# GpSimd scales the first head pair's softmax rows

## The chip, the core and the metric

One core of a Trainium2 chip runs one launch of the kernel. The metric is the time of the launch on the device in microseconds (us). The engines are TensorE (PE, with its weight loads as PEld), VectorE (DVE), ScalarE (ACT), GpSimd (POOL) and SyncE (SP, which here only issues DMAs).

## The reference, cut to what matters

One layer of a hybrid trunk is computed for 512 new frames of one stream and 64 next frames of a running one. Half of the heads are a state-space scan (SSD), the other half are latent attention (MLA), and a dense feed-forward network (FFN) follows. The change lies in the softmax of the attention:

```python
def block(args):
    ql, qr, qp = args
    s = (jnp.einsum('bqhl,bkl->bhqk', ql, keys_c, preferred_element_type=jnp.float32)
         + jnp.einsum('bqhr,bkr->bhqk', qr, keys_r, preferred_element_type=jnp.float32))
    mask = k_chunk[None, :] <= (qp // CHUNK)[:, None]
    s = jnp.where(mask, s * scale, -jnp.inf)
    pr = jax.nn.softmax(s, axis=-1).astype(keys_c.dtype)
    return jnp.einsum('bhqk,bkl->bqhl', pr, keys_c)
...
o = jnp.einsum('bthl,lhd->bthd', o_lat, p['w_uv']).reshape(b, T, MLA_WIDTH)
x = x + jnp.concatenate([y_ssd, o], axis=-1) @ p['w_out']
```

## The kernel before

The kernel runs through stages in one program: input projections and convolution, the SSD chunks, the attention, the output projection, the FFN and the final norm. Tokens lie on the free axis for most tensors (512 and 64, side by side), channels on the partitions.

In the attention the eight heads are worked in four pairs `p` (0 to 3). For a pair, `scores(p, i)` makes the scores of query block `i`: blocks 0 to 3 are 128 prompt queries each against `(i + 1) * 128` keys, one PSUM bank per head (`sc`, three banks in turn); block 4 (`sc_s`) is the 64 sample queries of both heads in one bank against 320 keys. `soft` then does four steps per head `j`: VectorE finds the negated row maximum from PSUM (L655), ScalarE exponentiates from PSUM into the SBUF tile `pr` and adds up the row sums (L656), VectorE takes the reciprocals of the sums of both heads in one instruction (L657), and the rows are multiplied by the reciprocal: head 0 by VectorE (L662), head 1 by ScalarE (L660). The exponential frees the PSUM bank for the next scores. `turn` then transposes `pr` on TensorE (`ptp`, L694), which needs the scaled rows of the query blocks that it covers, and `values` multiplies by V (`pv`, L719).

Around the first pair, which is the one that the diff touches, other work is interleaved: the second halves of the y norm (`nr_u`, `Ry`, L172 to L179), the gated SSD output scaled and split into `cat_y` for the output projection (L764, L143, L145), the splitting of the next pair's weights (`wl_pair`, L112) and copies of the next pair's queries (`qs`, L622). GpSimd has masked the SSD decay tiles (`cumb`, L515) before, and next issues the four DMAs that put the rotary part of pair 2's queries in place (`qs<-rrp`, L616).

The order of the work on each engine is written out: `ORDER_ATT` sets the order in which the pieces are made (S03 is block 3 of pair 0; the first pair goes S03, S01, S02, S00, S04), and `ISSUE` lists for each engine the numbers of its instructions in the order in which they are to be issued; `issue_in_order` turns that list into dependencies. The tiles of row sums and maxima (`sm`, `mx`) have four buffers, so the fifth block, S04, takes the buffer of S03, and the first block of pair 1 that of S01.

Of the kernel before, what the change touches and what calls it, by code (L numbers as in the profile page):

```python
# [14 lines left out]
ALU = mybir.AluOpType  # L15
# [39 lines left out]
def hybrid_layer_kernel(ctx: ExitStack, tc: tile.TileContext, a, o):  # L55
# [592 lines left out]
    def soft(p, i, scs, nk):  # L648
# [676 lines left out]
98-99 93-97 70-73 86-91 104-106 100-103 110 107-109 122-126 134-135 111-115 128-133 148-153 116-121 136-141 127  # L1325
142-147 154-169 174-175 170-171 270-274 176-221 172-173 222-269 275-370 373-420 371 421-468 372 469-634 637 641-644
638-640 657-660 635-636 665-726 737-758 661-664 763 645-652 759-760 727-736 764-766 653-656 767-818 859 761-762
819-826 860-864 833-840 827-832 865-870 841-852 871-874 853-856 875-880 857-858 881-887 904-912 888 892-899 889-891
900-903 925-926 913-921 927-934 922-924 935 939-940 936-938 949-957 964-966 941 945-948 967-968 958-963 969 942-944
970-975 987 976-979 1003 980-986 991-993 988 1004-1005 1015-1021 1006-1014 1022-1024 994-996 1025-1026 1029-1034  # L1330
1043-1045 997-998 989 1000-1002 999 1046-1054 990 1035-1039 1059-1061 1040-1042 1062-1064 1027-1028 1075-1077
1081-1092 1055-1057 1078-1080 1093-1096 1058 1097-1104 1121-1123 1071-1072 1124-1129 1065 1068-1070 1073 1105-1107
1066-1067 1074 1130-1156 1119-1120 1229-1240 1157 1108-1114 1158 1241-1245 1253-1262 1246-1247 1115-1118 1159-1161
1176-1177 1248-1252 1263-1264 1162-1175 1265 1180 1178 1181-1183 1179 1266-1268 1277-1279 1184-1187 1190-1195
1269-1276 1196-1204 1188-1189 1205-1223 1227-1228 1224-1226 1280-1297 1301-1303 1298-1300 1304-1321 1342-1343
1348-1355 1344-1347 1322-1341 1356-1511 1572 1512-1559 1575-1576 1560-1571 1577 1596-1598 1578 1573-1574 1593
1584-1585 1579 1581-1583 1602-1604 1623-1625 1594-1595 1614 1586 1605-1606 1590-1592 1611-1613 1632-1634 1587-1589
1608-1610 1607 1580 1599-1601 1620-1622 1641 1626-1628 1647-1649 1642-1643 1615-1616 1635-1637 1617-1619 1638-1640
1653 1656 1658-1667 1644-1646 1629-1631 1650-1652 1654-1655 1668-1669 1657 1682 1694-1705 1683-1693 1670-1681
1730-1741 1706-1729 1742-1748 1754-1755 1749-1753 1756-1767 1778-1785 1768-1777 1786-1885 1898-1905 1886-1897  # L1340
1906-2017 2030-2036 2018-2029 2037-2053 2066-2084 2054-2065 2085-2089 2102-2104 2090-2101 2105-2221 2234-2236
2240-2241 2222-2233 2237 2242-2248 2238-2239 2249-2725 2738-2740 2744 2726-2737 2741 2745-2751 2742-2743 2752-3229
3242-3244 3248 3230-3241 3245 3249-3255 3246-3247 3256-3733 3746-3748 3752 3734-3745 3749 3753-3759 3750-3751
3760-4189
# [5 lines left out]
101-102 125 120 126-127 119 131-133 155 134 129 135-136 140-142 149 104 152 128 150 153 170 143-144 138 145 147 151  # L1350
154 156 137 146 174 157 178 159 171-172 187 169 160 158 161-162 176 206 163 175 183 180 164 167 165-166 168 215 181
177 188 173 189 182 184 190 195 191 179 192-194 197 185-186 224 196 204 207-209 198-203 214 205 210 288 211 225
216-218 212 220 222 219 213 226 221 223 227-228 233 229-230 234 231-232 235-236 245 255 246 237 294 256 247 239 248
257 259 258 260 240 238 264 241 261 242 263 262 307 267 243 265 244 266 249 268 270 251 269 253 250 274 252 254
275-276 289 271 290 277-279 295 286 280 282 281 287 272 297 317 291 283 318 273 298 302 299 316 300 284-285 319 303
306 292-293 296 309 312 304 326 305 310 308 313 327 362 311 328 322 301 323 314 363 330 324 320 329 315 336 321 325
364 333 367 337 331-332 365 340 338 334-335 341 344 349 339 350 345 342 346 352 351 343 355 358 366 347 359 357 348
360 356 353 361 368 377 354 370-371 369 372 375-376 373-374 382 390 378 384 383 385-386 379 389 387 380 397 388 381
393 405 395 391 396 394 392 400 399 401 398 403 402 420 406 404 408 407 409 412 410 417 414 411 413 418 462 416 421
423 419 464 425 422 424 415 433 431 426 432 429 428 427 438 430 434 469 463 436 435 437 439 442 441 443 466 440 444  # L1360
451 465 446 467-468 452-453 445 447 455 454 448 473 475 456 477 476 474 457 472 470 478 458-459 449-450 479 460 481
480 461 471 482 491 487 483 496-497 484 488 498-499 489 500-502 485-486 503 510 490 515-518 522 492 504 519 506 520
507 521 508 532-535 539 546 493-495 536 547-549 505 511-512 509 523 537 529-530 524-525 513-514 531 538 540 528 550
541 566 526 542 527 551 543 545 552 544 567-568 553-554 569 555 574 570 556-559 561 575-576 560 565 577 562 578-581
571 582-583 572 563 590-591 584 592 585-586 564 598 573 599-600 593-594 587-588 601 589 603 602 595 604-607 596 610
597 608-609 620-623 611 627 612 624 613-614 625-626 619 634-636 628 637 617 638 618 629 616 615 630 641 639 631 640
633 632 654-656 642 657 643 662 658 644-647 649 663-664 648 653 665 650 666-669 659 670-671 660 651 678-679 672 680
673-674 652 686 661 687-688 681-682 675-676 689 677 691 690 683 692-695 684 698 685 696-697 708-711 699 715 700 712
701-702 713-714 707 722-724 716 725 705 726 706 717 704 703 718 729 727 719 728 721 720 742-744 730 745 731 750 746
732-735 737 751-752 736 741 753 738 754-757 747 758-759 748 739 766-767 760 768 761-762 740 774 749 775-776 769-770  # L1370
763-764 777 765 779 778 771 780-783 772 786 773 784-785 796-799 787 803 788 800 789-790 801-802 795 810-812 804 813
793 814 794 805 792 791 806 817 815 807 816 809 808 830-832 818 833 819 839 834 820-823 825 840-841 824 829 842 826
843-846 835 847-848 836 827 855-856 849 857 850-851 828 864 837 865-866 858 838 859 852-853 867 854 869 868 860
870-873 861 876 862 874 880 875 881-883 887 884 863 885 877 886 879 878 888-898
""",
    "ACT": """
0-5 8 6-7 10 9 13 11 14 12 15 17-18 16 21 19 24 20 23 40 22 25 45 26-27 52 28-33 49-50 56 34-35 37 36 60 51 41-43
38-39 64 44 46-48 53-54 68 55 57-58 72 59 61-62 76 63 65-67 77 69-71 73 92 74-75 94 79 88 78 81 104 82 90 84 116 86-87
103 85 83 100 98 80 97 89 99 102 101 96 91 126 105 93 111 109-110 156 115 95 107-108 113 122 114 112 142 117 163 106
118-119 136 127 137 134 128 140 135 124 121 120 139 129 138 141 130 123 143 131 125 150 146 149 132 210 133 145 148  # L1380
154 152 151 147 158-159 157 144 155 160-162 153 164-165 212 170 172 171 166 168 180 186 169 181 174 187 175 173 176
189 167 190 177 227 178 192 179 193 188 182 195 194 191 183 200 196 184-185 199 201 197 213 208 215-216 202-203 219
209 204 217 234 218 198 205-206 211 214 226 220 233 221 240 207 223 242 224 222 241 229 243-244 225 271 235 230 228
231 238 237 272 232 245 236 248 239 246 249-252 247 257 255 261 254 262 256 259 263 258 278 265 253 267 266 264
268-270 260 273-277 284 280-282 285 287 283 279 293 286 291 288 290 289 302 292 294 296 295 298 300 297 301 303-304
299 309 305-306 310 307 312 329 308 311 316-317 313-315 330 318 331 319-320 332 336 321-325 333 337 335 334 326 338
340 339 327 346 343 328 344 355-356 341-342 347-348 357 349 358 350 363 352 351 353 345 354 372 359 373 360-361
374-375 382-383 364-370 384 371 376 362 381 385 380 386 377 379 378 390-392 388 387 389 393 401 394 402 395 400 397
399 396 409 398 410 403 418-419 405-408 411 420 413 421 414-415 412 416-417 404 422 427 424 428 423 425-426 435-436
429 444-445 431-433 430 434 437 446 438 447 440-441 439 442-443 448 456-457 449 458 450 454 451 455 453 452 459 464  # L1390
460 465-466 462 461 463 467 475 468 476 469 474 471 473 470 483 472 484 477 492-493 479-482 485 494 487 495 488-489
# [117 lines left out]
```

## Time and profile before

| | |
|---|---|
| median of 3 runs | 635.12 us (634.90 to 635.19) |
| the profiled execution | 634.82 us, of which the span from the first to the last instruction is 633.1 us |
| PE busy | 622.9 us (98%), mean granted clock 0.997 |
| DVE busy | 541.9 us (86%) |
| ACT busy | 400.0 us (63%) |
| POOL busy | 110.9 us (18%), DMA issues included |

TensorE is busy for nearly the whole span, so the time falls only where TensorE waits, or where it has less to do. Of the span, 1.7 us lie outside (634.82 less 633.1). In the stretch from 151 to 161 us TensorE is busy for 8.31 of 10 us by its records, VectorE for 9.94, ScalarE for 9.39 and GpSimd for 1.96; the softmax of the first head pair lies there and just before.

### The profile page before, as it was taken

To read this page: it belongs to the slowest core of one execution; us is meant where nothing else is said; L and a number is where in the kernel's file an instruction comes from. 1 tells how busy PE (TensorE), PEld (TensorE's weight loads), DVE (VectorE), ACT (ScalarE), POOL (GpSimd) and SP (SyncE) were. 2 spreads that over 40 slices of the span, in tenths; PEclk is the share of its full clock that TensorE was granted. 3 is DMA by queue.
4 is the path that set the end of the run, shared out by engine and by line. 5 is a ranking of instruction groups with operands and counts; after the bars stand their busy time and mean duration, and the time that the engine had idled before them with its cause. 6 is when DMAs were issued, how large, how long until landed. Compare 5 with 4: busy or idle time off the path is not lost.

```text
span 633.1 us, 12089 instructions
## 1 busy us (share of the span) xinstructions
PE 622.9 (98%) x4635; PEld 596.2 (94%) x4635; DVE 541.9 (86%) x945; ACT 400.0 (63%) x768; POOL 110.9 (18%) x164
## 2 busy tenths in 40 slices
PE   9999999999999999999999999999999999999995
PEld 8899999886787899999999999999999999999995
DVE  6999986899776699999999888988899789976555
ACT  7655346779775567666556676566656665767364
POOL 1322103001010000001301330033104220323323
PEclk9999999999999999999999999999999999999998
DMA  8322364323231223335743986398738893689924
GB/s 320 135 61 74 96 198 122 113 75 102 81 117 34 95 73 126 88 113 172 260 131 89 217 182 156 79 191 186 172 100 161 198 204 101 101 215 256 254 38 149
DMA packets 39593, 89.19 MB, mean 141 GB/s; under 512 B 4570, under 2 KB 14312, under 8 KB 39280
## 3 DMA queue, kind: packets, MB, share of 16 engines
q1 hardware_dynamic: 26416, 63.12, 30.9%
q0 software_dynamic: 12400, 24.73, 21.4%
q8 instruction: 36, 0.59, 0.4%
q10 hardware_dynamic: 720, 0.57, 0.3%
q14 instruction: 21, 0.17, 0.1%
HBM read 62.74 MB, written 24.53 MB: 138 GB/s over the span
## 4 chain that ended last, share of the span: by engine, by line
PE 90%; DVE 5%; ACT 2%; issue 1%; POOL 1%; DMA 1%; POOLq 0%; DVEq 0%
PE ps_x L874 21%; PE ps_d L1064 14%; PE ps_z L874 10%; PE ps_in L281 8%; PE ps_o L458 5%; PE ps_y L874 5%; PE ps_z L458 4%; PE ps_first L129 3%; PE ps_d L281 2%; PE ps_p L874 2%; PE ps_l L281 2%; PE sc L672 2%; PE pv L719 1%; PE ptp L694 1%; PE ps_q L458 1%
## 5 line engine op out<-in xcount | busy, mean ns | idle before, releaser
L874 PE MATMUL ps_x<-xop,wh_gu_S 128*128 128x288 f32 x378 | 76.9, 295 | 0.0
L112 DVE TENSOR_TENSOR wl_gu_S<-gu,wh_gu_S 128x1024 fp32r<-128x1024 f32 x44 | 53.3, 1220 | 9.7 <-ACT wh_gu_S L111 6.5
L874 PEld LDWEIGHTS ps_x<-xop,wh_gu_S 128*128 128x128 f32 x378 | 60.5, 188 | 0.0
L1078 POOL DMA_DIRECT2D acc<-fz x32 | 27.9, 904 | 165.2 <-ACT fz L1075 136.5
L111 ACT CAST wh_gu_S<-gu 128x1024 fp32r<-128x1024 f32 x44 | 46.3, 1052 | 16.2 <-PE ps_y L874 8.3
L874 PE MATMUL ps_x<-xop,wl_gu_S 128*128 128x288 f32 x189 | 55.8, 295 | 0.0
L281 PE MATMUL ps_in<-xs,wh_in 128*128 128x256 f32 (+1 forms) x256 | 51.2, 296 | 0.4 <-DVE sp_a L361 0.4
L281 PEld LDWEIGHTS ps_in<-xs,wh_in 128*128 128x128 f32 x256 | 40.8, 188 | 1.2 <-issue 1.1
L281 PE MATMUL ps_in<-xs,wl_in 128*128 128x320 f32 (+1 forms) x128 | 37.7, 295 | 0.0
L874 PEld LDWEIGHTS ps_x<-xop,wl_gu_S 128*128 128x128 f32 x189 | 35.5, 188 | 0.0
L111 ACT CAST wh_gu_A<-gu 128x1024 fp32r<-128x1024 f32 x22 | 23.1, 1050 | 10.3 <-PE ps_x L874 6.9
L874 PE MATMUL ps_z<-xop,gu_a 128*128 128x288 f32 x189 | 29.5, 294 | 0.0
L458 PE MATMUL ps_o<-cat_y,wh_out 128*128 128x256 f32 (+1 forms) x128 | 29.0, 312 | 0.3 <-DVE cat_y L145 0.3
L112 DVE TENSOR_TENSOR wl_gu_A<-gu,wh_gu_A 128x1024 fp32r<-128x1024 f32 x22 | 26.8, 1218 | 1.2 <-ACT wh_gu_A L111 1.0
L874 PE MATMUL ps_x<-xop_last,wh_gu_S 128*128 128x288 f32 x126 | 26.9, 295 | 0.0
L874 PEld LDWEIGHTS ps_z<-xop,gu_a 128*128 128x128 f32 x189 | 26.5, 188 | 0.0
L1064 PE MATMUL ps_d<-pair,d_1h 128*128 128x288 f32 x128 | 26.4, 296 | 0.0
L874 PE MATMUL ps_z<-xop,wh_gu_S 128*128 128x288 f32 x126 | 26.0, 295 | 0.0
L458 PE MATMUL ps_z<-xs,wh_z 128*128 128x256 f32 (+1 forms) x128 | 25.8, 296 | 0.1
L458 PE MATMUL ps_o<-cat_o,wh_out 128*128 128x320 f32 (+1 forms) x128 | 25.5, 295 | 0.3 <-DVE x L750 0.3
L874 PE MATMUL ps_y<-xop,wh_gu_A 128*128 128x288 f32 x126 | 25.8, 296 | 0.0
L874 PE MATMUL ps_x<-xop,wh_gu_A 128*128 128x288 f32 x126 | 25.7, 295 | 0.0
(417 smaller groups left out, 2138.9 us busy)
## 6 DMA issues: line engine op xcount, KB each, us to landing
gu<-in_w_gu SPq DMA_DIRECT2D x44, 512.0 KB, 5.5
wr_d<-in_w_down SPq DMA_DIRECT2D x18, 512.0 KB, 4.0
acc<-fz POOLq DMA_DIRECT2D x16, 288.0 KB, 6.8
acc<-da POOLq DMA_DIRECT2D x16, 288.0 KB, 8.1
acc<-dc POOLq DMA_DIRECT2D x16, 288.0 KB, 8.6
wr_in<-in_w_in SPq DMA_DIRECT2D x8, 512.0 KB, 3.7
wr_out<-in_w_out SPq DMA_DIRECT2D x8, 512.0 KB, 3.3
cumb<-cumD SPq DMA_DIRECT2D x5, 512.0 KB, 4.5
```

The costliest lines, as they stand in the source:

```text
L111: act.copy(hi, raw)
L112: dve.tensor_tensor(lo, raw, hi.bitcast(F32), ALU.subtract)
L129: pe.matmul(ps[:m, hf, : cols.stop - cols.start], w, x[:, cols], start=start and k == 0 and i == 0, stop=stop and k == last and i == 2,)
L281: pe.matmul(ps, w, x[:, cols], start=first and k == 0 and i == 0, stop=last and k == len(terms) - 1 and i == 2,)
L458: pe.matmul(ps[:, :n], w, x[:, cols], start=k == 0 and i == 0, stop=k == len(terms) - 1 and i == 2,)
L672: pe.matmul(s[:, :nk], qs[:, j, q0 : q0 + P], ks[:, j, :nk], start=True, stop=True)
L694: pe.transpose(pp[:, k : k + P], prs[p, i][:, j, b * P : b * P + P], ident)
L719: pe.matmul(pv[64 * j : 64 * j + 64, b * P :], V[b][:, h * HD : (h + 1) * HD], pts[p, b, j], start=b == 0, stop=True, skip_group_check=b > 0,)
L874: pe.matmul(ps, p, q, start=not onto and first and kp == kps[0] and j == 0, stop=onto or (last and kp == kps[-1] and j == 2), skip_group_c ...
L1064: pe.matmul(ps, p, v, start=not onto and n == 0 and j == 0, stop=onto or (n == len(ks) - 1 and j == 2), skip_group_check=onto,)
L1078: pool.dma_start(out, src, accum_op=ALU.add)
```

## The change

The eight multiplications of pair 0's blocks 0 to 3 (four on VectorE, four on ScalarE) become eight GpSimd instructions. The sample block of pair 0 and all blocks of pairs 1 to 3 stay as they are.

```diff
         dve.reciprocal(sm[:, :n], sm[:, :n])
         for j in range(n):
-            if j:
+            if p == 0 and i < 4:
+                pool.tensor_scalar(pr[:, j], pr[:, j], sm[:, j : j + 1], None, ALU.mult)
+            elif j:
                 act.activation(pr[:, j], pr[:, j], AF.Identity, scale=sm[:, j : j + 1])
             else:
                 dve.tensor_scalar(pr[:, j], pr[:, j], sm[:, j : j + 1], None, ALU.mult)
...
 ISSUE = {
...
     "POOL": """
-0-3 7 18 28 4 8 5 9 6 10 26 11 27 12 29 13-17 20-23 19 24-25 31 30 32-42 53 55 57 59 54 56 58 60 43-52 61-69 71 73 75
...
+0-3 7 18 28 4 8 5 9 6 10 26 11 27 12 29 13-17 20-23 19 24-25 31 30 32-42 53 55 57 59 54 56 58 60 43-52 61-77 79 81 83 78
```

The numbers in `ISSUE` are counted anew, since three engines have other numbers of instructions; the order of all instructions that both kernels have is the same on every engine.

GpSimd, between the masking of the last SSD chunks (`cumb`) and the DMAs of the queries of pairs 2 and 3 (`qs`); the number right behind `pr` is the query block, `x2` its two heads, each an instruction:

```order
 L515 AFFINE_SELECT cumb_1598<-cumb_1598 128x1024
 L515 AFFINE_SELECT cumb_1716<-cumb_1716 128x1024
+L660 TENSOR_SCALAR pr_3_1946<-pr_3_1946,sm 128x512 x2
+L660 TENSOR_SCALAR pr_1_1972<-pr_1_1972,sm 128x256 x2
+L660 TENSOR_SCALAR pr_2_1986<-pr_2_1986,sm 128x384 x2
+L660 TENSOR_SCALAR pr_0_2000<-pr_0_2000,sm 128x128 x2
 L616 DMA qs_381<-rrp 16x576 x4
 L616 DMA qs_383<-rrp 16x576 x4
```

The eight scalings now stand on this engine ahead of those DMAs.

VectorE, in the softmax of pair 0's blocks 3, 1 and 2 and the y norm (`nr_v`, `nr_u`):

```order
 L657 RECIPROCAL sm<-sm 128x2
 L173 TENSOR_SCALAR nr_v<-R_98 128x288
-L662 TENSOR_SCALAR pr_3_1946<-pr_3_1946,sm 128x512
 L657 RECIPROCAL sm<-sm 128x2
 L655 TENSOR_REDUCE mx<-sc_2_0_1980 128x1
-L662 TENSOR_SCALAR pr_1_1972<-pr_1_1972,sm 128x256
 L655 TENSOR_REDUCE mx<-sc_2_1_1982 128x1
 L178 TENSOR_TENSOR nr_u<-nr_u,nr_v 128x288
```

Two of the four removed instructions stand here; the other two (blocks 2 and 0) are taken out in the same way a little later, and nothing takes their places.

ScalarE, between the last exponential of block 0 and the first `cat_y`:

```order
 L656 ACTIVATE pr_0_2000,sm<-sc_0_1_1996,mx 128x128
-L660 ACTIVATE pr_1_1972<-pr_1_1972,sm 128x256
-L660 ACTIVATE pr_3_1946<-pr_3_1946,sm 128x512
 L656 ACTIVATE pr_4_2013,sm<-sc_s,mx 128x320
-L660 ACTIVATE pr_0_2000<-pr_0_2000,sm 128x128
-L660 ACTIVATE pr_2_1986<-pr_2_1986,sm 128x384
 L143 ACTIVATE cat_y_1955<-xsd 128x576
```

All four of ScalarE's scalings of the pair stood around the exponential of the sample block, and are gone.

## Rows read from the trace of the kernel before

**Rows 1.** The profile page: busy time of the engines, share of the span.

```profile
PE 622.9 (98%) x4635; PEld 596.2 (94%) x4635; DVE 541.9 (86%) x945; ACT 400.0 (63%) x768; POOL 110.9 (18%) x164
```

**Rows 2.** The chain that ended last, 149 to 163 us: start, us, what.

```profile
149.28 0.46 ACT pr L656 x2
...
149.77 0.17 DVE sm L657
...
150.39 0.26 DVE pr L662
...
151.12 0.36 DVE nr_u L178
...
152.30 0.36 DVE Ry L179
...
153.14 0.16 DVE pr L662
...
153.38 0.55 DVE wl_pair L112
...
154.33 0.36 DVE nr_u L178
...
155.19 0.20 DVE pr L662
155.39 0.73 DVE xsd L764
...
159.93 0.68 DVE cat_y L145
...
160.65 2.28 PE ps_o L458 x15
```

**Rows 3.** Timeline of ACT, 153 to 157 us.

```profile
153.53 0.43 ACT L175 ACTIVATE nr_u<-nr_y 128x288 f32<-128x288 f32 x1
...
154.11 0.20 ACT L656 ACTIVATION_READ_ACCUMULATOR pr<-sc,mx 128x1 f32 x1
154.21 1.11 ACT L660 ACTIVATE pr<-pr,sm 128x256 f32<-128x256 f32 x2
...
155.72 0.90 ACT L660 ACTIVATE pr<-pr,sm 128x128 f32<-128x128 f32 x2
```

**Rows 4.** GpSimd: groups by line and shape (busy us, mean ns), then a timeline row.

```profile
L243 POOL TENSOR_SCALAR_AFFINE_SELECT ks<-ks 4x1664 f32<-4x1664 f32 x2 | 3.2, 1578 | 0.0
...
L243 POOL TENSOR_SCALAR_AFFINE_SELECT qs<-qs 4x1152 f32<-4x1152 f32 x2 | 2.3, 1152 | 0.1
...
610.05 0.88 POOL L1222 TENSOR_TENSOR fz<-fz,sq 128x320 f32<-128x320 f32 x1 [13.73 <-ACT sq L1217]
```

**Rows 5.** VectorE and GpSimd at once, 108 to 111 and 611 to 613 us: timeline rows.

```profile
108.49 1.09 POOL L515 TENSOR_SCALAR_AFFINE_SELECT cumb<-cumb 128x1024 f32<-128x1024 f32 x1 [6.30 <-ACT el L490]
...
108.58 0.49 DVE L468 SCALAR_TENSOR_TENSOR zh<-ps_z,R 128x320 f32<-128x320 f32 x1 [2.55 <-PE ps_z L458]
108.99 1.14 DVE L112 TENSOR_TENSOR wl_uv<-wr_uv,wh_uv 128x512 fp32r<-128x512 f32 x1
...
611.01 1.02 POOL L1222 TENSOR_TENSOR fz<-fz,sq 128x320 f32<-128x320 f32 x1
...
611.94 0.49 DVE L1227 TENSOR_TENSOR sq_last<-sq_last,sq 128x320 f32<-128x320 f32 x1
...
612.10 1.07 POOL L1222 TENSOR_TENSOR fz<-fz,sq 128x320 f32<-128x320 f32 x1
```

**Rows 6.** Timeline of DVE, 148 to 150 us.

```profile
148.97 0.29 DVE L173 TENSOR_SCALAR nr_v<-R 128x288 f32<-128x288 f32 x1
```

**Rows 7.** The DMAs behind the scalings: POOL's timeline, PE's timeline, DMA issues (landing).

```profile
153.06 2.02 POOL L616 DMA_DIRECT2D qs<-rrp  x4 [24.56 <-PE sc_s L678]
...
173.71 2.10 PE L672 MATMUL sc<-ks,qs 100*128 100x512 f32 x6
...
qs<-rrp POOLq DMA_DIRECT2D x16, 36.0 KB, 4.1
```

More of the change, by code (lines that the diff above doesn't have):

```diff
@@ L1329 @@
[L1329 to L1343, printed above, removed]
@@ L1344 @@
-3760-4189
+98-99 93-97 70-73 86-91 104-106 100-103 110 107-109 122-126 134-135 111-115 128-133 148-153 116-121 136-141 127 142-147
+154-169 174-175 170-171 270-274 176-221 172-173 222-269 275-370 373-420 371 421-468 372 469-634 637 641-644 638-640
+657-660 635-636 665-726 737-758 661-664 763 645-652 759-760 727-736 764-766 653-656 767-818 859 761-762 819-826 860-864
+833-840 827-832 865-870 841-852 871-874 853-856 875-880 857-858 881-887 904-912 888 892-899 889-891 900-903 925-926
+913-921 927-934 922-924 935 939-940 936-938 949-957 964-966 941 945-948 967-968 958-963 969 942-944 970-975 987 976-979
@@ new lines @@
+1003 980-986 991-993 988 1004-1005 1015-1021 1006-1014 1022-1024 994-996 1025-1026 1029-1034 1043-1045 997-998 989
+1000-1002 999 1046-1054 990 1035-1039 1059-1061 1040-1042 1062-1064 1027-1028 1075-1077 1081-1092 1055-1057 1078-1080
+1093-1096 1058 1097-1104 1121-1123 1071-1072 1124-1129 1065 1068-1070 1073 1105-1107 1066-1067 1074 1130-1156 1119-1120
+1229-1240 1157 1108-1114 1158 1241-1245 1253-1262 1246-1247 1115-1118 1159-1161 1176-1177 1248-1252 1263-1264 1162-1175
+1265 1180 1178 1181-1183 1179 1266-1268 1277-1279 1184-1187 1190-1195 1269-1276 1196-1204 1188-1189 1205-1223 1227-1228
@@ new lines @@
+1224-1226 1280-1297 1301-1303 1298-1300 1304-1321 1342-1343 1348-1355 1344-1347 1322-1341 1356-1511 1572 1512-1559
+1575-1576 1560-1571 1577 1596-1598 1578 1573-1574 1593 1584-1585 1579 1581-1583 1602-1604 1623-1625 1594-1595 1614 1586
+1605-1606 1590-1592 1611-1613 1632-1634 1587-1589 1608-1610 1607 1580 1599-1601 1620-1622 1641 1626-1628 1647-1649
+1642-1643 1615-1616 1635-1637 1617-1619 1638-1640 1653 1656 1658-1667 1644-1646 1629-1631 1650-1652 1654-1655 1668-1669
+1657 1682 1694-1705 1683-1693 1670-1681 1730-1741 1706-1729 1742-1748 1754-1755 1749-1753 1756-1767 1778-1785 1768-1777
@@ L1345 @@
+1786-1885 1898-1905 1886-1897 1906-2017 2030-2036 2018-2029 2037-2053 2066-2084 2054-2065 2085-2089 2102-2104 2090-2101
+2105-2221 2234-2236 2240-2241 2222-2233 2237 2242-2248 2238-2239 2249-2725 2738-2740 2744 2726-2737 2741 2745-2751
+2742-2743 2752-3229 3242-3244 3248 3230-3241 3245 3249-3255 3246-3247 3256-3733 3746-3748 3752 3734-3745 3749 3753-3759
+3750-3751 3760-4189
 """,
@@ L1354 @@
[L1354 to L1363, printed above, removed]
@@ L1374 @@
-870-873 861 876 862 874 880 875 881-883 887 884 863 885 877 886 879 878 888-898
+101-102 125 120 126-127 119 131-133 155 134 129 135-136 140-142 149 104 152 128 150 153 170 143-144 138 145 147 151 154
+156 137 146 174 157 178 159 171-172 187 169 160 158 161-162 176 206 163 175 183 180 164 167 165-166 168 215 181 177 188
+173 189 182 184 190 195 191 179 192-194 197 185-186 224 196 204 207-209 198-203 214 205 210 284 211 225 216-218 212 220
+222 219 213 226 221 223 227-228 233 229-230 234 231-232 235-236 245 254 246 237 290 255 247 239 256-258 240 238 261 241
@@ new lines @@
+259 242 260 303 263 243 262 244 248 264 266 250 265 252 249 270 251 253 271-272 285 267 286 273-275 291 282 276 278 277
+283 268 293 313 287 279 314 269 294 298 295 312 296 280-281 315 299 302 288-289 292 305 308 300 322 301 306 304 309 323
+358 307 324 318 297 319 310 359 326 320 316 325 311 332 317 321 360 329 363 333 327-328 361 336 334 330-331 337 340 345
+335 346 341 338 342 348 347 339 351 354 362 343 355 353 344 356 352 349 357 364 373 350 366-367 365 368 371-372 369-370
+378 386 374 380 379 381-382 375 385 383 376 393 384 377 389 401 391 387 392 390 388 396 395 397 394 399 398 416 402 400
@@ new lines @@
+404 403 405 408 406 413 410 407 409 414 458 412 417 419 415 460 421 418 420 411 429 427 422 428 425 424 423 434 426 430
+465 459 432 431 433 435 438 437 439 462 436 440 447 461 442 463-464 448-449 441 443 451 450 444 469 471 452 473 472 470
+453 468 466 474 454-455 445-446 475 456 477 476 457 467 478 487 483 479 492-493 480 484 494-495 485 496-498 481-482 499
+506 486 511-514 518 488 500 515 502 516 503 517 504 528-531 535 542 489-491 532 543-545 501 507-508 505 519 533 525-526
+520-521 509-510 527 534 536 524 546 537 562 522 538 523 547 539 541 548 540 563-564 549-550 565 551 570 566 552-555 557
@@ new lines @@
+571-572 556 561 573 558 574-577 567 578-579 568 559 586-587 580 588 581-582 560 594 569 595-596 589-590 583-584 597 585
+599 598 591 600-603 592 606 593 604-605 616-619 607 623 608 620 609-610 621-622 615 630-632 624 633 613 634 614 625 612
+611 626 637 635 627 636 629 628 650-652 638 653 639 658 654 640-643 645 659-660 644 649 661 646 662-665 655 666-667 656
+647 674-675 668 676 669-670 648 682 657 683-684 677-678 671-672 685 673 687 686 679 688-691 680 694 681 692-693 704-707
+695 711 696 708 697-698 709-710 703 718-720 712 721 701 722 702 713 700 699 714 725 723 715 724 717 716 738-740 726 741
@@ new lines @@
+727 746 742 728-731 733 747-748 732 737 749 734 750-753 743 754-755 744 735 762-763 756 764 757-758 736 770 745 771-772
+765-766 759-760 773 761 775 774 767 776-779 768 782 769 780-781 792-795 783 799 784 796 785-786 797-798 791 806-808 800
+809 789 810 790 801 788 787 802 813 811 803 812 805 804 826-828 814 829 815 835 830 816-819 821 836-837 820 825 838 822
+839-842 831 843-844 832 823 851-852 845 853 846-847 824 860 833 861-862 854 834 855 848-849 863 850 865 864 856 866-869
+857 872 858 870 876 871 877-879 883 880 859 881 873 882 875 874 884-894
@@ new lines @@
+136 127 137 134 128 140 135 124 121 120 139 129 138 141 130 123 143 131 125 150 146 149 132 206 133 145 148 154 152 151
+147 158-159 157 144 155 160-162 153 164-165 208 170 172 171 166 168 180 185 169 181 174 186 175 173 176 187 167 188 177
+223 178 189 179 190-191 182 196 192 183-184 195 197 193 209 204 211-212 198-199 215 205 200 213 230 214 194 201-202 207
+210 222 216 229 217 236 203 219 238 220 218 237 225 239-240 221 267 231 226 224 227 234 233 268 228 241 232 244 235 242
+245-248 243 253 251 257 250 258 252 255 259 254 274 261 249 263 262 260 264-266 256 269-273 280 276-278 281 283 279 275
@@ new lines @@
+289 282 287 284 286 285 298 288 290 292 291 294 296 293 297 299-300 295 305 301-302 306 303 308 325 304 307 312-313
+309-311 326 314 327 315-316 328 332 317-321 329 333 331 330 322 334 336 335 323 342 339 324 340 351-352 337-338 343-344
+353 345 354 346 359 348 347 349 341 350 368 355 369 356-357 370-371 378-379 360-366 380 367 372 358 377 381 376 382 373
+375 374 386-388 384 383 385 389 397 390 398 391 396 393 395 392 405 394 406 399 414-415 401-404 407 416 409 417 410-411
+408 412-413 400 418 423 420 424 419 421-422 431-432 425 440-441 427-429 426 430 433 442 434 443 436-437 435 438-439 444
@@ new lines @@
+452-453 445 454 446 450 447 451 449 448 455 460 456 461-462 458 457 459 463 471 464 472 465 470 467 469 466 479 468 480
+473 488-489 475-478 481 490 483 491 484-485 482 486-487 474 492 497 494 498 493 495-496 505-506 499 514-515 501-503 500
+504 507 516 508 517 510-511 509 512-513 518 526-527 519 528 520 524 521 525 523 522 529 534 530 535-536 532 531 533 537
+545 538 546 539 544 541 543 540 553 542 554 547 562-563 549-552 555 564 557 565 558-559 556 560-561 548 566 571 568 572
+567 569-570 579-580 573 588-589 575-577 574 578 581 590 582 591 584-585 583 586-587 592 600-601 593 602 594 598 595 599
@@ L1408 @@
+67 65 76 69-71 78 73 86 64 74-75 87 80 88-89 84 90 85 91 98 101 99-100 102-103 106-165
 """,
```

53 lines of the change are left out of this document (9 added, 44 removed).

## Prediction

> **What bounds the kernel now.** The page comes first: TensorE is busy for 98% of the span [rows 1], so an edit on other engines moves the time only through a wait of TensorE. The reader then looks at the chain that ended last, in the stretch where the edited instructions stand. Up to 149.74 it is ScalarE's, in the exponentials; from 149.77 to 160.61 us every piece of it is VectorE work, and it is handed to TensorE at 160.65, when the second `cat_y` split has ended [rows 2]. From there on the chain is almost all TensorE. So the question is when VectorE reaches the end of the `cat_y` splits. Three of VectorE's four edited scalings are pieces of that chain (0.26, 0.16 and 0.20 us); the fourth, of block 3, lies before 149.77, where VectorE waits for ScalarE's row sums anyway. ScalarE's four scalings (two in the 1.11 us at 154.21, two in the 0.90 us at 155.72 [rows 3]) are no piece of the chain: their 2.0 us are worth something only if ScalarE's results come late to VectorE, and from 149.77 to 160.61 the chain has no ScalarE piece.
>
> **What the removal is worth.** On the chain 0.26 + 0.16 + 0.20 = 0.62 us go. Not all of it arrives. The multiplication `nr_u` (L178) that the chain has at 154.33 needs ScalarE's square, which ends at 153.53 + 0.43 = 153.96, and the reciprocal of block 0 behind it needs the row sums of 154.11 + 0.20 = 154.31 [rows 3]; neither is moved by this change, since ScalarE's scalings stand behind them. Up to that point VectorE could be 0.42 us early (0.26 + 0.16), but the instructions can move by about 0.26 only. Behind it the 0.20 of block 0 come whole. By this alone the first `xsd` scaling (L764, whose piece runs from 155.39 to 156.12), and all that follows in order, comes 0.46 us earlier: a ceiling for the gain.
>
> **What GpSimd takes.** No row shows a tensor_scalar on GpSimd. The nearest rows are its masks, which also read one tensor and write one: 1152 elements take 1152 ns and 1664 take 1578 [rows 4], so (1578 - 1152) / 512 = 0.83 ns an element and about 0.19 us for the instruction. That prices the scalings at 0.62 us (512 elements), 0.51 (384), 0.41 (256) and 0.30 (128), two each: 3.7 us in all. The dear end is its addition of two tensors, 0.88 us for 320 elements [rows 4], or 2.75 ns an element with everything in it: 1.41, 1.06, 0.70 and 0.35, 7.0 us in all. I take the cheap end, since a scaling has one tensor input too, and keep both for the range. By the Trainium skill ("GPSIMD Engine Reference", section 3.1) a tight loop on one input takes 769 ns for 512 elements, 1.5 ns each. An estimate at that price, walked like the two below, would put the time at about +0.9 us instead of the +0.3 that follows; no row here shows it.
>
> **What GpSimd and VectorE do to each other.** This is the term that speaks against the change. A weight split of 128x384 takes 0.55 us on the chain [rows 2], so 128x512 should take some 0.7; it took 1.14 when it began at 108.99, while a GpSimd mask ran from 108.49 to 109.58. It was held until the mask ended. VectorE's instruction just before, with one operand in PSUM, ran 0.49 us beside the same mask [rows 5], and that is what 320 elements take at 611.94 too. Both directions show at 612 us: VectorE's addition of two SBUF tensors at 611.94 met the end of a GpSimd addition (611.01 + 1.02 = 612.03) and ran its usual 0.49, and GpSimd's next, issued at 612.10, took 1.07 instead of 0.88. So they take turns, an instruction at a time, also between two GpSimd instructions that stand back to back. The Trainium skill ("SBUF — State Buffer", section "Who interferes with whom") has the same as a rule: a VectorE instruction with two SBUF inputs, or in a two-port mode, and a GpSimd instruction that reads SBUF exclude each other, while an instruction with a PSUM input does not take part. The trace agrees with that rule.
>
> On the chain from 149.77 to 156.12 the instructions with two SBUF inputs are `nr_u` (twice), `Ry`, `wl_pair` and the first `xsd`; the row maxima and the `qs` copy read PSUM. I walk it with the cheap prices. The `nr_v` behind block 3's reciprocal ends at 149.26 [rows 6], and I let GpSimd begin there (`nr_v`, with one SBUF input, is counted as excluding too; if it doesn't, 0.2 us are gained at most). GpSimd scales block 3 until 150.50, while VectorE has only PSUM work, and block 1's first head until 150.91. `nr_u` wants to begin then. If GpSimd's second head goes first, `nr_u` waits until 151.32 and ends at 151.72 (0.24 late against 151.48); if VectorE goes first, it ends at 151.38 (0.10 early). Some issue gaps on the way absorb up to 0.2 of lateness. Block 2's reciprocal comes near 152.6 to 152.9; its first scaling follows a `nr_v` and ends at 153.34 to 153.65. `wl_pair`, early by the removed 0.16 and more, wants to begin near 153.0 to 153.2, waits for that end, and is done at 153.84 to 154.15 (before: 153.93). The second head of block 2 then holds the second `nr_u` until 154.35 to 154.66, and its end is 0.05 to 0.36 late. Block 0's scalings wait for `Ry`, the first ends at 155.55 to 155.85 and holds the first `xsd`, which ends at 156.30 to 156.60 instead of 156.12.
>
> **The sum.** So the removed 0.62 us are given back in waits on the shared access: +0.17 to +0.48 us at the point from which VectorE's order runs on unchanged, and I take +0.3. The remaining pieces up to 160.60 meet only the last scaling of block 0, beside a reciprocal and a row maximum from PSUM. The transposes of block 0 stand ready on TensorE from about 156.2, and their first rows are scaled by 155.9, the second head's by 156.9, before it is read. Behind 160.65 everything shifts as one. The profiled execution takes 634.82, so 635.1; the median of the runs, 635.12, lies 0.3 above it, which makes **635.4**. Measurements of this kernel can tell a difference of about 0.2%, 1.27 us, from none: the forecast is no change.
>
> **Costed at nothing.** The four DMA issues for pair 2's queries, 2.02 us from 153.06, now stand behind the scalings. If the last scaling ends at 156.9, they end near 158.9, and with 4.1 us to land the queries are in place at 163.0; pair 2's scores begin in the piece at 173.71 [rows 7]. The cover is 10 us; without it TensorE would wait one for one. The four `sm` buffers make the exponential of the sample block wait until GpSimd has read block 3's sums (150.5, or 152.1 at the dear price, against a start after 154.2), and pair 1's first exponential until block 1's are read: hidden in both. ScalarE's 2.0 us free the sample block's bank earlier and let TensorE do pair 1's scores sooner, but what it does next waits for VectorE's chain.
>
> **Rivals.** *No holding* (0.12): VectorE keeps its 0.46, for instance because scalings by a column read differently from the masks. Then 635.12 - 0.46 = 634.7, still no measurable change; the 1.14 us row speaks against it.
>
> *The dear price* (0.13), the rival on the slower side: a scaling takes as long per element as the addition of two tensors, and each is a longer hold. Walked as above, `nr_u` waits for block 3's second scaling (until 152.06, 1.1 us), `Ry` hardly at all, `nr_v` 0.6 for block 1, `wl_pair` 0.85 and the second `nr_u` 0.75 for block 2, `xsd` 0.4 for block 0: 3.7 us, less at most 0.62 removed, +3.1, so 638.2 at the far end. On a straight line between the two walks (0.62 us for 512 elements, 1.21 ns each, gives +0.3, and 2.75 gives +3.1) the measurable 1.27 is passed at about 1.75 ns, or 0.9 us for 512 elements: from there this rival decides.
>
> *ScalarE's time comes through* (0.03): if the chain that I read as VectorE's is in truth ScalarE's for the exponentials, up to 2.0 us could be won, 633.1. The chain has no ScalarE piece after 149.75, and even a ScalarE piece would meet the next VectorE wait.
>
> **How the numbers follow.** The forecast, a net shift between -0.3 (part of the holds missed) and +0.9 us (a fifth of the way to the dear walk), so 634.8 to 636.0, has 0.70; no holding 0.12, the dear price 0.13, ScalarE's gain 0.03, and 0.02 for what I don't see. No change is 0.70 + 0.12 and half of the last, 0.83; slower 0.13, faster 0.04. The range that holds 8 in 10 covers the forecast and no holding with a margin of 0.2 below, and half of the way to the dear end above (+1.7): 634.5 to 636.8.
>
> **What would show it.** Right: eight GpSimd instructions of L660 from 149.1 to about 157, those of 512 elements near 0.6 us; VectorE's pieces of `nr_u`, `wl_pair` and `xsd` longer than 0.36, 0.55 and 0.73 us; TensorE reaching `ps_o` of the second `cat_y` within 0.5 us of 160.65; later stages shifted by the same amount. Wrong: scalings of 1.2 us or more for 512 elements, TensorE waiting for GpSimd at `ptp`, or a chain that has GpSimd pieces in it.

## The result: slower by 0.4%, outside the range

The changed kernel takes 637.79 us in the median of six runs (636.35 to 638.56), against 635.15 for the kernel before on the same chip (634.90 to 635.39): a ratio of 1.0040, with an interval of 1.0027 to 1.0053. So it is 2.6 us slower, and this is more than the measurement's noise. Two further jobs gave 638.00 (ratio 1.0034, 1.0022 to 1.0047) and 637.16 (1.0028, 1.0018 to 1.0039). Over the 20 runs of the three jobs the median is 637.6, some 2.4 us above the kernel before, and single runs lie between 635.9 and 638.8: they are spread wider than those of the kernel before.

The profiled execution of the changed kernel took 637.51 us, with a span of 635.8. The page's busy times, which answer to [rows 1]:

```profile
PE 626.1 (98%) x4635; PEld 598.3 (94%) x4635; DVE 541.9 (85%) x941; ACT 398.8 (63%) x764; POOL 121.2 (19%) x172
```

VectorE lost four scalings and is as busy as before; GpSimd gained eight instructions and 10.3 us. The line of the scalings in the trace after (all eight, shortest, median and longest in ns; then who waited for them, us and times), and four of the eight in GpSimd's timeline (start, us):

```profile
L660 POOL TENSOR_SCALAR pr<-pr,sm x8: 821/1346/1832, 149.6 to 158.3; 128x512 f32<-128x512 f32 x2, 128x256 f32<-128x256 f32 x2, 128x384 f32<-128x384 f32 x2, 128x128 f32<-128x128 f32 x2
...
  PEld ptp L696: 1.8, 2
  PE ptp L696: 0.3, 1
...
149.55 1.57 POOL L660 TENSOR_SCALAR pr<-pr,sm 128x512 f32<-128x512 f32 x1 [20.82 <-DVE nr_v L173]
151.12 1.83 POOL L660 TENSOR_SCALAR pr<-pr,sm 128x512 f32<-128x512 f32 x1
...
157.45 0.82 POOL L660 TENSOR_SCALAR pr<-pr,sm 128x128 f32<-128x128 f32 x1
158.25 1.45 POOL L660 TENSOR_SCALAR pr<-pr,sm 128x128 f32<-128x128 f32 x1
```

A scaling of 512 elements takes 1.57 or 1.83 us, not 0.62, and the queue is over at 159.70 us, not 156.9. The chain that ended last, where [rows 2] had VectorE from 149.77 to 160.61, now reads (start, us):

```profile
151.12 4.18 POOL pr L660 x4
...
157.45 2.26 POOL pr L660 x2
...
159.76 1.12 PE ptp L696 x4
...
162.58 2.72 PE ps_o L458 x21
```

It is GpSimd's, and it goes to TensorE at the transposes of the first pair (`ptp`), not at the output projection. These are the second four, of head 1; from 159.76 on every piece of the chain is TensorE's own work, one behind the other, since the transposes stand ahead of the scores (`sc`) and of the projection in its order. In the kernel before, the same transposes began at 157.47, and TensorE waited once more, 0.31 us, for VectorE's `cat_y` at 160.65; after the change no wait for `cat_y` is recorded there. TensorE before (a row of its timeline, a piece of the chain), then the chain after:

```profile
157.47 0.60 PE L694 MATMUL ptp<-ident,pr 128*128 128x128 f32 x4
...
163.56 0.80 PE ps_q L458 x6
```

```profile
165.93 0.80 PE ps_q L458 x6
```

ScalarE comes late behind the first transposes too. Its timeline after:

```profile
156.23 0.68 ACT L143 ACTIVATE cat_y<-xsd 128x576 fp32r<-128x576 f32 x1 [1.25 <-DVE xsd L766]
159.48 0.59 ACT L698 COPY pt<-ptp 128x512 f32<-128x512 f32 x1 [2.56 <-PE ptp L696]
159.96 0.69 ACT L656 ACTIVATE pr<-sc,mx 128x512 f32<-128x512 f32 x1
...
160.64 1.82 ACT L143 ACTIVATE cat_y<-xsd 128x576 fp32r<-128x576 f32 x3
```

ScalarE stands 2.56 us before the copy `pt` that empties the first transposes. In its queue an exponential and the remaining three `cat_y` stand behind that copy, although they don't need it, and VectorE's second halves of `cat_y` and TensorE's `ps_o` need those. In the kernel before, the same copy began at 157.26; it is 2.2 us later now. In this profile that is no piece of the chain, because TensorE itself comes to `ps_o` no sooner. The first `ps_q` behind the projection begins at 165.93 instead of 163.56, 2.4 us later. From there to 612 us both traces run in step; the last 0.3 of the 2.7 us between these two profiles come behind that.

### The profile page after: what moved, and what is told of

Its sections match the earlier page's. It is cut to its first block, busy times and chain, and to the rows that moved or that the text cites. A ratio compares the mean times of both kernels' runs of the same rounds, so it can differ in the third digit from the quotient of the medians.

```text
span 635.8 us, 12096 instructions
## 1 busy us (share of the span) xinstructions
PE 626.1 (98%) x4635; PEld 598.3 (94%) x4635; DVE 541.9 (85%) x941; ACT 398.8 (63%) x764; POOL 121.2 (19%) x172
## 4 chain that ended last, share of the span: by engine, by line
PE 88%; DVE 5%; ACT 2%; issue 2%; POOL 2%; DMA 1%; POOLq 0%; DVEq 0%
PE ps_x L876 21%; PE ps_d L1066 14%; PE ps_z L876 10%; PE ps_in L281 7%; PE ps_y L876 5%; PE ps_o L458 4%; PE ps_z L458 4%; PE ps_first L129 3%; PE ps_d L281 2%; PE ps_p L876 2%; PE sc L674 2%; PE ps_l L281 2%; PE pv L721 1%; PE ptp L696 1%; POOL pr L660 1%
## 5 line engine op out<-in xcount | busy, mean ns | idle before, releaser
L111 ACT CAST wh_gu_A<-gu 128x1024 fp32r<-128x1024 f32 x22 | 23.1, 1050 | 10.3 <-PE ps_x L876 6.9
L1025 POOL DMA_DIRECT2D acc<-dn x8 | 4.4, 544 | 121.5 <-ACT dn L1024 121.5
```

The source lines that it names most:

```text
L111: act.copy(hi, raw)
```

## The experiments

Three theories were set against each other. **Theory 1** (price and wait): a scaling on GpSimd costs some 2.5 times the forecast, and TensorE waits at its first transposes for the last two, those of block 0. **Theory 2** (holding): GpSimd and VectorE take turns at memory, and what VectorE loses by that is the cost. **Theory 3** (clock): around the wait the granted clock of TensorE falls from 2.4 to 1.2 GHz (0.50 in the rows), and that is the cost. Except where something else is said, a kernel is timed in 10 or 11 runs (the repetitions of the changed kernel in 6 and 8), beside the kernel before on the same chip.

**Part of the change.** Five kernels leave some of the scalings where they were. The edit is the condition; `ISSUE` is counted anew.

```diff
-            if p == 0 and i < 4:
+            if p == 0 and i in (3, 1):
```

> Four of the eight scalings stay on GpSimd, those of prompt blocks 3 and 1; blocks 2 and 0 are scaled as before the change. Theory 1 (price: a scaling on GpSimd takes 1.57 us at 512 columns, and TensorE waits at the first transposes for the last ones, blocks 2 and 0): the four pieces are over at about 154.9 us, ahead of the transposes at 156.3, so nothing waits; VectorE loses 0.42 us of its own scalings; 634.7 to 635.2 us, -0.1 to -0.4 against before. Theory 2 (holding: GpSimd and VectorE take turns at memory while both work): the same four run beside VectorE's recip-and-update work, so a good half of the loss stays, about +1.2 us, 636.3. Theory 3 (TensorE's granted clock in this stretch): no wait, so no drop; as theory 1.

```diff
-            if p == 0 and i < 4:
+            if p == 0 and i < 4 and j == 0:
```

> Only head 0's four scalings (those that VectorE made before) on GpSimd, head 1's on ScalarE as before. Theory 1: the four take 1.57, 0.9, 1.3 and 0.6 us, GpSimd is done at about 155.3 us, a microsecond ahead of the first transpose; VectorE is 0.62 us lighter on the chain, so 634.7 us (-0.4, bounds -0.6 and 0). Theory 2: about +1.2 us, 636.3, since half of GpSimd's work lies beside VectorE's. Theory 3: as theory 1.

With `j == 1` in its place:

> Only head 1's four scalings (those that ScalarE made before) on GpSimd, head 0's on VectorE as before. Theory 1: GpSimd is done at about 155.5 us, ahead of the transposes; VectorE's chain is what it was; 635.1 us, within 0.3 of before. Theory 2: +1.2 us. Theory 3: as theory 1. Against the run with head 0 alone it shows whether ScalarE's 2.0 us come through: if this one is the faster by over 0.3 us, they do.

With `i in (3, 1, 2)`:

> Six of the eight on GpSimd, blocks 3, 1 and 2; block 0 as before the change. Theory 1: GpSimd is done at about 157.4 us, 1.1 us after TensorE could begin the transposes of block 0 and about when it comes to those of the later blocks; between no loss and +1.5, taken +0.7 us, 635.9. Theory 2: three quarters of the loss, +1.9 us, 637.0. Theory 3: with a wait of TensorE the drop follows, +1.5 to +2.4.

And with all but the last in GpSimd's queue, `i < 4 and (i or not j)`:

> Seven of the eight scalings on GpSimd; only block 0, head 1 (128 columns, the last in GpSimd's queue) is made by ScalarE as before. Theory 1: GpSimd is done at 158.3 us instead of 159.7; the run with six, done at 157.5, lost nothing and the one with eight lost 2.7, so about +0.8 to +1.2 us, 636.0 to 636.5. Theory 2 (the loss comes from all that GpSimd holds of VectorE): seven eighths of the loss, +2.3, 637.6.

What was measured, in order of the end of GpSimd's last scaling in the profile of each:

| on GpSimd | last scaling ends (us) | median (us) | ratio to before |
|---|---|---|---|
| blocks 3 and 1 (four) | 154.5 | 635.12 | 0.9998 (0.9989 to 1.0007) |
| head 0 (four) | 155.5 | 635.23 | 0.9999 (0.9990 to 1.0008) |
| head 1 (four) | 155.6 | 635.60 | 1.0004 (0.9995 to 1.0013) |
| blocks 3, 1, 2 (six) | 157.5 | 635.24 | 1.0001 (0.9992 to 1.0009) |
| all but block 0, head 1 (seven) | 158.4 | 636.79 | 1.0021 (1.0013 to 1.0030) |
| all eight | 159.7 | 637.79, 638.00, 637.16 | 1.0040, 1.0034, 1.0028 |

Six scalings and 7.95 us of GpSimd's time beside VectorE cost nothing that is measured; the seventh, of 128 columns, costs 1.4 us. So the loss doesn't grow with the work that GpSimd does beside VectorE, as it should by theory 2; it begins when the queue ends at some point between 157.5 and 158.4 us. With seven, the last scaling is the one that TensorE's first four transposes read, and the chain of that profile goes on through ScalarE's copy and exponentials to the next scores (start, us):

```profile
158.46 0.67 PE ptp L696 x4
...
159.15 0.02 ACT pt L698
...
159.63 0.79 ACT pr L656 x2
...
160.47 0.91 PE sc L674 x2
```

I had expected less for seven (+0.8 to +1.2) and more for six (+0.7). The two halves by head differ by 0.4 us within their intervals: it doesn't matter measurably whether VectorE or ScalarE is relieved.

**The removal alone.** The statement becomes `pass`, so the prompt blocks of the first pair are not divided by their sums.

> The eight scalings are left out on every engine, so the prompt blocks of the first head pair are not divided by their sums. This is the removal alone, the term that the prediction put at -0.46 us. Theories 1, 2 and 3: 634.7 us (-0.3 to -0.6). If the time is that of before, the removal was worth nothing; if it is 1 us or more below, ScalarE's part comes through.

635.01 us, ratio 0.9995 (0.9986 to 1.0004). The 0.46 us of the prediction fit into the interval (0.9 us less to 0.3 more), and so does nothing at all; that is all there is to win from these eight scalings, and none of the versions beats the kernel before by what can be measured. In the profile of this kernel the granted clock fell to 0.50 from about 154.4 to 157.9 us, and the first transposes came at 157.8 with it, yet this execution took 635.23 us, 0.2 above the median of its kernel: there the low clock cost little, and it fell in a kernel that has no scaling on GpSimd to wait for.

**The same work, read by nobody.** GpSimd writes into a spare tile, and the prompt blocks of the first pair stay undivided.

```diff
-                pool.tensor_scalar(pr[:, j], pr[:, j], sm[:, j : j + 1], None, ALU.mult)
+                pool.tensor_scalar(idle[:, :nk], pr[:, j], sm[:, j : j + 1], None, ALU.mult)
```

> GpSimd makes the eight scalings into a tile that nobody reads, and no engine scales the probabilities themselves, so the prompt blocks of the first head pair are not divided by their sums. The same memory traffic of GpSimd beside VectorE, but nobody waits for it. Theory 1 (price and wait): the time of the kernel without the eight, 634.7 us, within 0.3 of it. Theory 2 (holding): as slow as the changed kernel, 637.5 us, since VectorE is held as it was.

635.72 us, ratio 1.0007 (0.9998 to 1.0015), although GpSimd's last scaling ends at 160.8 us here. So what GpSimd does to VectorE can't make the 2.4 us; the wait must be for its result. The same run rules out two other ways of losing: here too the row sums are read late, and the DMAs behind the scalings are issued from 160.8 us. Against the removal alone it is 0.0012 more in the ratios, some 0.8 us with intervals of about as much, where theory 1 allowed 0.3. A hold of VectorE is seen in this kernel's chain (start, us), to be read beside the pieces of [rows 2]:

```profile
152.75 0.70 DVE wl_pair L112
...
153.85 0.52 DVE nr_u L178
...
154.90 1.02 DVE xsd L767
...
160.48 2.38 PE ps_o L458 x15
```

0.70, 0.52 and 1.02 us stand where 0.55, 0.36 and 0.73 stood; what they have grown by adds up to 0.60, uses up what the removal gave, and TensorE gets the second `cat_y` about when it did.

**A constant instead of the column.** All eight by 0.01 (not divided by their sums).

```diff
-                pool.tensor_scalar(pr[:, j], pr[:, j], sm[:, j : j + 1], None, ALU.mult)
+                pool.tensor_scalar(pr[:, j], pr[:, j], 0.01, None, ALU.mult)
```

> All eight scalings on GpSimd, but by the constant 0.01 in place of the column of inverse sums, so that the rows are not divided by their sums. Told for the price of the column: if the operand costs, 512 columns take nearer 0.6 us (the mask's 0.83 ns an element) and the time is about 635.3; if the price is the operation's own, 1.3 to 1.8 us and 637.5 us.

635.38 us, ratio 0.9999 (0.9991 to 1.0008): the time of the first case with the durations of the second, 0.52 to 2.23 us. Neither case held as put. The operand isn't the price (128 elements take 0.52 us here and 0.61 with the column, below), but without the reciprocal to wait for the queue begins at 147.8 instead of 149.6 and ends at 157.1, ahead of the second transposes (157.3; TensorE waits 0.21 us for GpSimd at the first, which begin at 156.69); so this kernel belongs in the table above, just ahead of the six, and fits it.

**The price by itself.** Into the kernel before, eleven scalings are put that nobody needs.

```diff
+    spare = qk_bufs[1][1][:, 0]
+    pool.memset(spare[:, :512], 1.0)
+    for w in (512, 128, 256, 512, 384, 256, 128, 512, 384, 256, 128):
+        pool.tensor_scalar(spare[:, :w], spare[:, :w], ones[:100, :1], None, ALU.mult)
```

> The kernel before, with eleven scalings that nobody needs put at the head of GpSimd's queue (on 100 rows of a buffer not yet in use, by a column of ones): widths 512, 128 and 256 in the first 5 us, where VectorE has hardly begun, then 512, 384, 256 and 128 twice, beside VectorE's splits of the input. It tells what a scaling costs alone and what beside VectorE. Theory 1: alone 1.5, 0.52 and 0.85 us (0.2 us and 2.5 ns an element), so that GpSimd's own price makes 8.1 of the 10.15 us of the change. Theory 2: alone about 0.6 us for 512 (0.83 ns an element, the forecast's), and all the rest is VectorE's hold on it.

They began at 22 us and not in the first 5, because the buffer's place was in use by another tile until then, and what GpSimd does there came later by as much (646.9 us in a single run; its time tells nothing else). The last four ran where VectorE had almost no work, and one of 512 ran where it worked all the time, on a split of two SBUF tensors (1.21 us) and then on products with one operand in PSUM. GpSimd's timeline (start, us), then two stretches (length; busy time of PE, PEld, DVE, ACT, POOL; granted clock, DMA share, GB/s):

```profile
26.32 2.63 POOL L242 TENSOR_SCALAR ks<-ks,ones 100x512 f32<-100x512 f32 x1
...
32.10 1.57 POOL L242 TENSOR_SCALAR ks<-ks,ones 100x512 f32<-100x512 f32 x1
...
33.76 1.25 POOL L242 TENSOR_SCALAR ks<-ks,ones 100x384 f32<-100x384 f32 x1
...
35.10 0.93 POOL L242 TENSOR_SCALAR ks<-ks,ones 100x256 f32<-100x256 f32 x1
...
36.12 0.61 POOL L242 TENSOR_SCALAR ks<-ks,ones 100x128 f32<-100x128 f32 x1
...
26.30:29.00 2.70, 2.70 (x26) 1.44 (x24) 2.70 (x5) 0.78 (x2) 2.63 (x1) 1.00 0.13 24
31.40:36.80 5.40, 5.40 (x45) 5.37 (x45) 0.41 (x1) 2.04 (x3) 4.96 (x6) 1.00 0.01 5
```

Alone, 512 elements take 1.57 us and 128 take 0.61: (1.57 - 0.61) / 384 = 2.5 ns an element and 0.29 us for the instruction. The eight cost 2 x (1.57 + 1.25 + 0.93 + 0.61) = 8.7 us by themselves; in the change they took 10.15. I put the 1.4 us down to VectorE, and then it is GpSimd that is held: 2.63 us instead of 1.57 in the worst row, beside a busy VectorE and little DMA (24 GB/s). In the change DMA runs at 250 to 434 GB/s from 155 to 159 us, where the last scalings take 0.82 and 1.45 us instead of 0.61; no run tells its part from VectorE's there.

**The wait or the clock.** The changed kernel was run again:

> The changed kernel again, for a second profile and more timed runs. Theory 1 (price): TensorE's first transposes again wait for GpSimd's last scalings, at about 158.3 and 159.7 us, 637.8 us. Theory 3 (clock): if the profile shows full granted clock from 154 to 162 us, its time is that of before; if it shows the drop, about +2.4.

> The changed kernel once more, on the same chip and in the same rounds as the two that follow, so that they can be compared with it: 637.8 to 638.0 us.

638.00 and 637.16 us, the second below what was expected. In both of these profiles TensorE stands still longer than in the first one, and the clock falls behind the wait, while in the first it fell ahead of it, at 154.8 us. PE in the second repetition, by stretch (length, busy, granted clock, DMA share, GB/s), and two rows of the first profile:

```profile
157.00:158.00 1.00, 0.00 (x0) 1.00 0.99 367
...
159.00:160.00 1.00, 0.45 (x5) 1.00 0.74 313
...
161.00:162.00 1.00, 1.00 (x6) 0.50 0.36 74
162.00:163.00 1.00, 1.00 (x3) 0.50 0.35 74
163.00:164.00 1.00, 1.00 (x6) 0.50 0.00 0
```

```profile
155.00:156.00 1.00, 1.00 (x3) 0.50 0.85 250
...
161.00:162.00 1.00, 1.00 (x7) 0.71 0.35 76
```

To take the low clock away and leave the wait, products that nobody reads were put on TensorE, into the PSUM bank that the transposes write next. First six, four ahead of the first four transposes and two ahead of the next four:

```diff
+            for _ in range((4, 2)[j] if p == b0 == 0 else 0):
+                pe.matmul(pp, qks[0][0][:, 0, :P], qks[0][1][:, 0, : 4 * P], start=True, stop=True)
```

> The changed kernel with six products of 512 columns added on TensorE that nobody reads, four ahead of the first transposes of head pair 0 and two between the first four and the next four, so that TensorE works where it waited for GpSimd (0.43 us each at full clock: 1.7 and 0.9 us, about the two waits). Theory 1 (TensorE waits for scalings that come late): the end of GpSimd's queue at 159.7 us still decides, 637.5 to 638.1 us. Theory 3 (what costs is the half clock that goes with the wait): the granted clock stays at 1.00 from 155 to 165 us and 1 to 2 us come back, 636.0 to 636.8. If the products themselves come out too long for the waits, it is up to 0.4 us slower than the changed kernel.

640.20 us, ratio 1.0068 (1.0054 to 1.0082), five runs. One product takes 0.86 us and not 0.43, so they ran past both waits, and TensorE's first transposes came at 161.6 us instead of 158.3. For the clock it says nothing, and little for the wait: these transposes are 5.0 us later than the 156.6 of the kernel before and the time is 4.9 us longer, but six products are 5.2 us of work on TensorE itself. With `(2, 1)` the products fit:

> As the run with six added products, but with three, since one of 512 columns was found to take 0.86 us: two ahead of the first four transposes (1.7 us) and one ahead of the next four (0.86 us), which fits the two waits of a run at full clock (156.9 to 158.6 and 159.2 to 160.0 us). Theory 1: the time of the changed kernel, 637.5 to 638.2 us, up to 639 where the clock falls before the products. Theory 3: no low clock behind the transposes, and 636.3 to 637.2 us; of the two profiles of the changed kernel, the one whose clock fell behind the wait took 0.7 us more than the one whose clock fell ahead of it, which is the most that theory 1 leaves to the clock.

636.75 us, ratio 1.0025 (1.0016 to 1.0034). The runs with a mean clock of 0.997 to 0.999 have a median of 636.3 (six), those of 0.994 and 0.995 one of 637.6 (five); the interval of the ratio overlaps with those of the changed kernel. Last, a fourth product of 448 columns was added where TensorE waits at 153.3 us in any case, and this one alone was put into the kernel before as the control:

> The changed kernel with three products of 512 columns in the two waits of TensorE for GpSimd and a fourth, of 448, in the 0.84 us for which TensorE waits at 153.3 us in the kernel before too; nobody reads them. If the half clock follows TensorE's waits, it now stays away in every run (mean clock 0.998 or 0.999) and what is left is the wait itself: 636.3 to 636.6 us, with less spread than 637.2 to 638.8. If the loss is the wait alone, it stays at 637.8.

> The kernel before the change with only the product of 448 columns added at 153.3 us, nobody reads it. Where the clock of the kernel before falls in some of its runs at 154.5 us, this takes it away: 634.9 to 635.2 us, 0 to 0.4 below before. It is the control: the filler without the change must not gain the 1.3 us that it gives back to the changed kernel.

636.44 us, ratio 1.0022 (1.0013 to 1.0031), against 637.16 and 1.0028 (1.0018 to 1.0039) for the changed kernel in the same job: the two intervals overlap. Three of the eleven runs stay above 637.2, where all were to come down, and two of these three show a mean clock of 0.997 and 0.998. It is 635.23 for the control, ratio 1.0002 (0.9993 to 1.0011). The granted clock is 1.00 in every stretch from 150 to 165 us in the profile with four products, GpSimd's last scaling still ends at 159.7, and the pieces of TensorE behind it compare as follows: of the changed kernel (second repetition), then with four products (start, us):

```profile
161.96 1.28 PE sc L674 x2
163.24 3.19 PE ps_o L458 x21
166.43 0.33 PE ptp L696 x3
```

```profile
159.98 0.44 PE ptp L698 x4
...
161.08 0.65 PE sc L674 x2
161.73 2.73 PE ps_o L458 x21
164.45 0.33 PE ptp L698 x3
...
165.08 0.80 PE ps_q L458 x6
```

From the end of the last scaling (160.05 and 159.71) to the end of these `ps_o` it is 6.4 us in the one and 4.7 in the other; in the first profile it is 5.6 (159.70 to 165.31). So by the profiles 0.9 to 1.6 us of the loss are TensorE's work at 1.2 GHz. The times don't tell this part from none: the products give back 0.7 us between the medians of the job that has both, and 1.1 against all 20 runs, which are from other chips too. With four products 1.2 us are left (636.44 less 635.20), the wait itself as far as these runs show it.

The same pieces tell how much lateness is free. From the end of the second transposes to `ps_q` it is 5.5 us in the kernel before (158.07 to 163.56) and 4.7 with four products (160.42 to 165.08), both at full clock. As an estimate from these two profiles, TensorE's other waits take up the first 0.8 us by which these transposes come late.

So theory 2 falls as the cause in the way it was put, by what VectorE loses; theory 1 has the place and the point at which the loss begins; theory 3 is a part of the loss in the profiled executions, from a third to nearly half of it, and is not shown in the medians.

What stays open: why the clock falls ahead of the wait in some executions and behind it in others, and what sets apart the runs of the changed kernel near 636 us from those near 638; their mean clocks don't (636.03 and 638.21 both show 0.996).

## Why the prediction was wrong

**The step that failed** is "What GpSimd takes", and in it the choice of the cheap end. 0.62 us were forecast for 512 elements, and alone it is 1.57. Even the end that I called dear (1.41) lay below it, so the bounds didn't bound: the addition takes 0.88 us for 320 elements, and a scaling, by 0.29 us and 2.5 ns an element, 1.09. By this estimate a multiplication with one tensor input is dearer here than an addition with two, and it is three times as dear by the element as a mask. Of all eight, 3.7 us were forecast and 7.0 called dear; it was 8.7 alone and 10.15 beside VectorE. The sentence that should have been the forecast was in the rivals: a time of 0.9 us or more for 512 elements decides. The Trainium skill's 769 ns for 512 elements ("GPSIMD Engine Reference", section 3.1), its best case of a tight loop, is half of what the eleven added scalings show for this operation, 1.57 us.

**"The transposes are hidden" fell with it.** The first of them begin at 156.6 us in the trace before (their weights are loaded from 156.31, near the 156.2 that I had), and I expected the second head's rows at 156.9. With the true price block 0, last in GpSimd's queue and first in TensorE's, ends at 158.3 and 159.7. So the path that I walked, VectorE's to the second `cat_y`, no longer decided: with all eight, TensorE's own order carries the wait from the second transposes through the scores to the projection. I didn't ask what stands behind a late transpose.

**The holding went the other way.** I let VectorE wait for GpSimd an instruction at a time and priced the change by it. In the trace after, `nr_u` begins at 151.13, a hundredth after a GpSimd scaling of 1.83 us, and takes 0.46 (0.45 before); `Ry` begins at 152.33, inside the same scaling, and takes 0.45 as before; `wl_pair` takes 0.62 (0.55), and only the first `xsd` is held much, 1.02 instead of 0.81. VectorE's last `xsd` ends at 160.08, against 159.92. GpSimd's instructions are the ones that get longer. The rule of the Trainium skill that I leaned on ("SBUF — State Buffer", "Who interferes with whom"), that the two exclude each other, with the one that issues first served first, holds for the mask of [rows 5] and not for these scalings: the measurement decides. The run with unread results is 0.4 us above the kernel before, near my +0.3 net, but its interval holds no loss too; if the size was right, it was so by another way than I reasoned, and it doesn't make the result.

**The rival "dear price"** had the sign, nearly the operation's price (1.41 against 1.57 us) and nearly the time (638.2), and the wrong path: it went through VectorE's waits, so that its time came close is luck. Its chance, 0.13, was set by a price that I had no row for.

**What was right:** the removal is worth little (0.46 us forecast as a ceiling, 0.3 measured, not told from nothing); ScalarE's 2.0 us come to nothing that is measured; the DMAs behind the scalings stay hidden (they are issued by 161.7 us, and pair 2's scores run at 176.3); and the signs of a wrong forecast that I named, 1.2 us for 512 elements, a TensorE that waits at `ptp` and GpSimd pieces in the chain, are all there.

**What the price alone would have done** no run shows. 8.7 us from 149.55 end at 158.3, near the 158.4 of the run with seven scalings (+1.4 us). But there the first transposes wait to the end of the queue; here it would be the second ones, and the first would have their rows at 157.7. So, as an estimate, the bare price costs less than 1.4 us, and the 1.4 us by which the queue is longer beside VectorE make a good part of the loss.

## What to carry to other kernels

Where the trace has no row for an operation on an engine, a row of another operation on it is no bound; if the forecast turns on that price, the range must reach as far as the point at which it decides, with a real chance. When work goes to a slower engine, add up its queue to the end and compare that with the first reader of the last result, and then read on each engine's order what stands behind that reader, needed or not. Lateness is free up to the waits that the reader's engine has anyway, here some 0.8 us. And a wait of TensorE can cost more than itself: in the profile of the second repetition 1.6 us came on top, from work behind it at the low clock.

## What the runs showed of the hardware that was not expected

GpSimd's multiplication by a column takes 0.29 us and 2.5 ns an element of fp32 (0.61 to 1.57 us for 128 to 512 columns, on 100 partitions), three times the mask's 0.83 by the element [rows 4]; by a constant 128 elements took 0.52. Beside a VectorE that was busy throughout, 512 elements took up to 2.63 us.

Three useless products on TensorE in its waits, 2.6 us of them, made the changed kernel no slower (636.75 us against 637.16, 637.79 and 638.00, in other jobs), and the granted clock stayed at 1.00 from 150 to 165 us in its profile. That they make it faster is not shown, since the intervals of the ratios overlap.

A transfer can lie near the same path. In the profile of the kernel with head 0 on GpSimd, an execution of 636.07 us, the chain has a load of the residual `x`, and TensorE waits for VectorE's addition behind it until 164.4 us:

```profile
154.15 9.67 DMA x<-in_xT
...
163.91 0.44 DVE x L752
...
164.39 1.06 PE ps_q L458 x6
```

This may be what spreads the runs of the kernels that don't wait for GpSimd (634.4 to 636.1), but no run here tests it.
